# A two-layer encoder on one core: the residual kept in DRAM during the mixers, a step's values prepared after the step before it, and the mixer's modulation moved beside the inversions

## The chip, the cores and the metric

The kernel runs on one core of one Trainium2 chip. The metric is the device time of one execution in microseconds; the median of 3 runs is 1579.02 us (1576.25 to 1579.44). The names of the engines are those of the profile: PE (TensorE, matmuls), PEld (its weight loads), DVE (VectorE), ACT (ScalarE), POOL (GpSimd), SP (the queue that issues nearly all DMAs).

## The reference

Two layers, each of a half-step feed-forward, a gated mixer of three branches, and another half-step feed-forward; D = 1024, 256 tokens, hidden width 2816. All weights are float32.

```
def reference(x, c, ...):
    cs = silu(c)
    for l in range(2):
        mod = cs @ ada_w[l] + ada_b[l]                  # 9 vectors of 1024: shift, scale, gate of 3 sub-layers
        h = modulate(rmsnorm(x), sh1, sc1)
        x = x + 0.5 * gt1 * swiglu(h, ffn_wi[l, 0], ffn_wo[l, 0])
        h = modulate(rmsnorm(x), sh2, sc2)
        x = x + gt2 * hybrid_mixer(h, ...)
        h = modulate(rmsnorm(x), sh3, sc3)
        x = x + 0.5 * gt3 * swiglu(h, ffn_wi[l, 1], ffn_wo[l, 1])
    return rmsnorm(x, final_norm)

def hybrid_mixer(h, ...):
    proj = h @ w_in[l]
    o_a = dilated_attention(rotary(aq), rotary(ak), av)     # 8 heads x 64
    o_b = neighborhood_attention(nq, nk, nv, rpb[l])
    o_c = rwkv7_bidirectional(pr, pk, pv, ...)              # a scan over the tokens in each direction
    merged = sum of sigmoid(gate_b) * (o_b @ w_branch[b])   # over the three branches
    return merged @ w_out[l]

def _rwkv_step(state, inp):
    r, w, k, v, a_vec, b_vec = inp
    sa = state . a_vec
    state = state * w + sa (x) b_vec + v (x) k
    y = state . r
```

## The kernel before

The residual `xT` holds x transposed, 8 tiles of 128 x 256, in SBUF for the whole run. Every product is computed with float32 weights cut in two float32r parts: ACT casts a piece of 128 x 512 weights (`whi`, L360), DVE subtracts to get the rest (`wlo`, L369), and PE runs three matmuls for each 128 x 128 tile (L404 to L406, "dense matmuls" below). Weights come through SP in 512 KB loads (`wraw`).

The modulation is not done on PE. For each of the 72 blocks of 128 outputs of a layer SP loads 512 KB (`araw`) and DVE multiplies and sums them in one pass (L468). These loads are started by a pace: during a mixer 24 of them (vectors 5, 7 and 6 of the layer: the mixer's gate, the next scale, the next shift), from START = 110 after the mixer's start in the planner's clock, every PACE = 7.

The order of all instructions is fixed when the kernel is built. Each activity is a generator (a thread); `Order.run` gives every engine its next instruction by planned times, priorities and counted resources (`take`, `release`, `wait`). At run time every engine runs its list in order, and what arrives later than planned holds everything behind it on that engine. `s_big` counts the shared buffers of one pool (tag "b4", NBIG = 34), `s_z` smaller ones (NZ = 10). Thread `main` issues the dense matmuls; all else fits in between.

In the mixer the third branch (RWKV) is the long chain. Tokens are cut in four chunks of 64 in each direction (steps n = 0 to 3). For each step `invert` builds the chunk's matrices (`pG` on PE, `G` on DVE), inverts 8 x 8 blocks (`blocks8`: one matmul `p` at L1228, then 14 small DVE operations in a row) and doubles the block size three times (`pX`, `pT`, L1181 and L1193, with a copy, a predicated copy and a transposition between). `values` prepares what the scan needs of v and b (`pBT`, `pvt`, `pMV`; tiles `uv`, `bu`). `scan` then does the step itself (`pAS`, `pU`, `pS1`, `pY`), and `post` normalises the output (`pvar`, `pgi`) into `oC`. Only then can the third branch's product (`oC`), W_out (`m`) and the residual's update run. Two threads of `invert` run over steps 0, 2 and 1, 3; each takes five shared buffers for a step before it begins (G twice, `uv`, `bu`, `tw`), and `uv` and `bu` are held from there to the step's end:

```
for _ in range(5 - (n == 3) + (n == ns[0])):
    yield take(s_big)
...
G = [big("G", (128, 2, 4, 128)) for _ in range(2)]
uv = big("uv", (128, 2, 8, 64))
bu = big("bu", (128, 2, 8, 64)) if n < 3 else None
tw = big("tw", (128, 2, 2, 4, 64))
```

Beside the chain `main` runs the dense products of the projections, of the first two branches and of the gates (input `h` or `o`).

Of the kernel before, what the change touches and what calls it, by code (L numbers as in the profile page):

```python
# [8 lines left out]
F32 = mybir.dt.float32  # L9
# [12 lines left out]
BIG = 1e30  # L22
TWO_PI_PARTS = (6.28125, 0.0019350051879882812, 3.0199159819e-07)
ROUND = 12582912.0
NBIG, NZ, NZ2 = 34, 10, 2
NRAW, NSPL, NADA, NPM = 3, 4, 2, 3
ORDER = "cabAgB"
NCK, NLR = 2, 2
WARM = 0
NJ0 = 8  # L30
NXF, NXM = 4, 8
PACE, START = 7, 110
FPACE, FSTART = 5, 12
WPRIO = -1
LAT, MM = {"PE": 0.2, "ACT": 0.15, "DVE": 0.13, "SP": 0.0}, 0.329
VPRIO = 4
# [125 lines left out]
def wait(ev):  # L162
    return ("wait", ev, 0, 0)
# [6 lines left out]
def take(sem, n=1):  # L170
    return ("take", sem, n, 0)
# [20 lines left out]
def trunk(ctx, tc, A, out):  # L192
# [21 lines left out]
    def big(name, shape=(128, 4, S), dt=F32):  # L214
        return act.tile(list(shape), dt, name=name, tag="b4", bufs=NBIG)
# [7 lines left out]
    def free_big(n=1):  # L223
        od.release(s_big, n)
# [4 lines left out]
        eng.dma_start(t, A[key])  # L229
        return t  # L230

    xT = act.tile([128, KT, S], F32, name="xT")
    csb = const.tile([128, D], F32, name="csb")
    cT = cload("cT", [128, KT], eng=nc.sync)
    ident = cload("ident", [128, 128], eng=nc.sync)
# [271 lines left out]
    def mod(l, v):  # L507
        return modT[l][:, v * 8:v * 8 + 8]
# [344 lines left out]
    def mixer(l, st):  # L853
        yield take(s_big, 4)
        ha = Act("h", KT)
        od.spawn(modulated(l, 1, st, ha), 0)
        vec = tmp.tile([128, 14, 4], F32, name="vec", bufs=1)
        mul = tmp.tile([128, 2], F32, name="mul", bufs=1)
        for t, src in ((vec[:, 0:13], "vec"), (mul, "mul")):
# [262 lines left out]

        e_inv, e_val = ([Event() for _ in range(4)] for _ in range(2))
        CH = {}
        s_ck = Sem(NCK)
        n_inv, e_got = [0], [Event() for _ in range(5)]

        def toks(c):
            return slice(c * 64, c * 64 + 64)
# [1 line left out]
        def invert(ns):  # L1131
            for e in e_ab:
                yield wait(e)
            for n in ns:
                cs = (n, 3 - n)
                if n > 0:
                    yield wait(e_got[n - 1])
                yield take(s_ck)
                for _ in range(5 - (n == 3) + (n == ns[0])):
                    yield take(s_big)  # L1140
                od.set(e_got[n])
                if n == ns[0]:
                    tx = big("tx", (128, 2, 2, 4, 64))
                    T, X = tx[:, 0], tx[:, 1]
                G = [big("G", (128, 2, 4, 128)) for _ in range(2)]
                uv = big("uv", (128, 2, 8, 64))
                bu = big("bu", (128, 2, 8, 64)) if n < 3 else None
                tw = big("tw", (128, 2, 2, 4, 64))
                TT, W1 = tw[:, 0], tw[:, 1]
                for d in range(2):  # L1150
                    yield take(s_px, 2)
                    pp = [paux("pG", (128, 4, 128)) for _ in range(2)]
                    yield on("PE", 1.3)
                    for i in range(4):
                        for b in range(2):
                            hs = half(b)
                            P.matmul(pp[b][:, i], BK[d][i // 2][hs, i % 2, cs[d]].rearrange("p a b -> p (a b)"),
                                     ar_view(d, i // 2)[hs, :, i % 2, toks(cs[d])], start=True, stop=True)
                    for b in range(2):
                        yield on("DVE", 0.6)  # L1160
                        V.tensor_mul(G[b][:, d], pp[b], mg[:, d][:, None, :].to_broadcast([128, 4, 128]))
                        od.release(s_px)
                yield from blocks8(G, X, TT)
                yield on("DVE", 0.6)
                flip(T, TT)
                od.spawn(values(n, cs, G, bu, uv, W1), VPRIO)
                for lv in range(3):
                    w = 8 << lv

                    def part_(t, d, a):  # L1170
                        return t[:, d].rearrange("p h c -> p (h c)").rearrange("p (x a s) -> p x a s", a=2, s=w)[:, :, a]

                    def halves_(t, a):
                        return skew(part_(t, 0, a), part_(t, 1, 1 - a))

                    yield take(s_px)
                    px = paux("pX", (128, 2, 4, 64))
                    yield on("PE", 0.85)
# [12 lines left out]
                    for d in range(2):  # L1191
                        for h in range(8):
                            P.matmul(pt[half(h), d, h // 2], X[half(h), d, h // 2], TT[half(h), d, h // 2], start=True, stop=True)  # L1193
                    yield on("DVE", 0.335)
                    V.copy_predicated(halves_(TT, 1), lvl[:, lv].rearrange("p d (x s) -> p d x s", s=w), halves_(pt, 1))
                    od.release(s_px)
                    if lv < 2:
                        yield on("DVE", 0.6)
                        flip(T, TT)
                CH[n] = (G, bu, uv, TT, W1)  # L1200
                yield wait(e_val[n])
                od.set(e_inv[n])
            n_inv[0] += 1
            free_big(1 if n_inv[0] == 1 else 5)

        def blocks8(G, m, TT):

# [36 lines left out]

            V.transpose(t.rearrange("p d a b -> p (d a b)"), tt.rearrange("p d a b -> p (d a b)"))

        def values(n, cs, G, bu, uv, W1):
            for d in range(2):
                yield wait(e_rkv[d, 2])
            if n < 3:  # L1250
                yield take(s_px, 2)
                p = [paux("pBT", (128, 2, 4, 64)) for _ in range(2)]
# [26 lines left out]
            yield from copy_any(W1, p, 512)  # L1279
            od.release(s_px)  # L1280
            od.set(e_val[n])

        e_y = {(d, t): Event() for d in range(2) for t in range(2)}

        def scan():
# [2 lines left out]
            yield take(s_big)  # L1288
            for n in range(4):
                cs = (n, 3 - n)  # L1290
                yield wait(e_inv[n])
                G, bu, uv, TT, W1 = CH[n]
                ar = lambda d, h, z: ar_view(d, h // 4)[half(h), z, h // 2 % 2, toks(cs[d])]
# [52 lines left out]
                od.release(s_px)  # L1346
                free_big(5 - (n == 3))
                od.release(s_ck)
                ST = sn
            free_big(5)  # L1350

# [382 lines left out]
        ha.free()  # L1734
        yield take(s_big, 4)
        ma = Act("m", KT)
        yield wait(e_oC)
        yield from branch(2, oC[0], gts)
        free_big(4)
# [2 lines left out]
        yield wait(have[l, 5])  # L1742
        yield on("DVE", 0.07)
        V.tensor_scalar(g, mod(l, 5), 0.5, None, op0=OP.mult)
        p3 = []
        for m in range(NPM):
            yield take(s_pm)
# [23 lines left out]
    def main():  # L1771
# [14 lines left out]
        for k in range(KT):  # L1786
            yield on("DVE", 0.34)
            V.tensor_mul(xT[:, k], xT[:, k], st.r)
            if k % 2 == 0 or k == KT - 1:
                k0 = max(k - 1, 0) if k < KT - 1 else k  # L1790
                nc.sync.dma_start(out[:, k0:k + 1], xT[:, k0:k + 1])

    od.spawn(main(), 7, True)
# [124 lines left out]
```

## Time and profile before

| | |
|---|---|
| median of 3 runs | 1579.02 us |
| the profiled execution | 1579.55 us, its span 1577.7 us |
| busy in that span | PE 1509.2, PEld 1440.4, DVE 1288.8, ACT 856.1 us |
| mixer of layer 0, from its first normalisation (217.7 us) to the next (612.4 us) | 394.7 us |
| mixer of layer 1, 992.8 to 1384.3 us | 391.5 us |
| first chunk matrices (`pG`) in these | 391.6 us and 1155.5 us |

A window's row gives its length, then for each engine the busy time and the number of instructions that began in it; PEclk is the granted TensorE clock as a share of its full speed (1.00 is 2.4 GHz, 0.50 is 1.2 GHz), then the mean busy share of the DMA engines and GB/s. The two mixers are each cut at their first `pG` into a head (projections, attention) and a tail (inversions, scan, third branch, W_out).

### The profile page before, as it was taken

To read this page: it belongs to the slowest core of one execution; us is meant where nothing else is said; L and a number is where in the kernel's file an instruction comes from. 1 tells how busy PE (TensorE), PEld (TensorE's weight loads), DVE (VectorE), ACT (ScalarE), POOL (GpSimd) and SP (SyncE) were. 2 spreads that over 40 slices of the span, in tenths; PEclk is the share of its full clock that TensorE was granted. 3 is DMA by queue.
4 is the path that set the end of the run, shared out by engine and by line. 5 is a ranking of instruction groups with operands and counts; after the bars stand their busy time and mean duration, and the time that the engine had idled before them with its cause. 6 is when DMAs were issued, how large, how long until landed. Compare 5 with 4: busy or idle time off the path is not lost.

```text
span 1577.7 us, 36363 instructions
## 1 busy us (share of the span) xinstructions
PE 1509.2 (96%) x14470; PEld 1440.4 (91%) x14470; DVE 1288.8 (82%) x2732; ACT 856.1 (54%) x1730; POOL 2.3 (0%) x22
## 2 busy tenths in 40 slices
PE   6999999999899989999999999999999987999997
PEld 6998999979689879999999999998888977999997
DVE  8888789989768688988789877999897687998664
ACT  4556457566344347555565545676654433665554
POOL 0000000000000000000000000000000000000000
PEclk9999999999899969999999999999999988999999
DMA  9687864446223435887668885543652352457553
GB/s 345 215 301 269 277 224 162 163 147 234 100 95 133 135 139 196 274 289 262 221 208 278 276 273 195 189 159 129 219 165 100 122 190 106 146 202 267 188 187 121
DMA packets 96226, 311.58 MB, mean 197 GB/s; under 512 B 11444, under 2 KB 22964, under 8 KB 96056
## 3 DMA queue, kind: packets, MB, share of 16 engines
q1 hardware_dynamic: 95768, 309.15, 57.8%
q8 instruction: 113, 1.85, 0.5%
q14 instruction: 57, 0.47, 0.1%
q10 hardware_dynamic: 288, 0.10, 0.0%
HBM read 308.17 MB, written 1.05 MB: 196 GB/s over the span
## 4 chain that ended last, share of the span: by engine, by line
PE 88%; DVE 6%; DMA 3%; issue 1%; ACT 1%; SPq 1%; DVEq 0%; ACTq 0%
PE pmain L404 21%; PE pmain L405 20%; PE pmain L406 20%; DMA araw<-in_ada_w_dram 3%; PE pearly L404 2%; PE pearly L406 2%; PE pearly L405 2%; PE pX L1181 1%; DVE araw L468 1%; PE pT L1193 1%; PE pS L1499 1%; PE pfirst L405 1%; PE pfirst L406 1%; PE pfirst L404 1%; DVE wlo L369 1%
## 5 line engine op out<-in xcount | busy, mean ns | idle before, releaser
L360 ACT CAST whi<-wraw 128x512 fp32r<-128x512 f32 x828 | 508.5, 619 | 444.6 <-PE pmain L405 291.8
L369 DVE TENSOR_TENSOR wlo<-wraw,whi 128x512 fp32r<-128x512 f32 x828 | 566.6, 689 | 118.0 <-ACT whi L360 108.0
L404 PE MATMUL pmain<-h,whi 128*128 128x256 f32 x1840 | 528.1, 287 | 0.0
L405 PE MATMUL pmain<-h,whi 128*128 128x256 f32 x1840 | 517.4, 281 | 0.0
L406 PE MATMUL pmain<-h,wlo 128*128 128x256 f32 x1840 | 515.6, 280 | 0.0
L404 PEld LDWEIGHTS pmain<-h,whi 128*128 128x128 f32 x1840 | 346.1, 188 | 12.2 <-issue 8.2
L406 PEld LDWEIGHTS pmain<-h,wlo 128*128 128x128 f32 x1840 | 347.4, 189 | 0.3 <-DVE wlo L369 0.2
L405 PEld LDWEIGHTS pmain<-h,whi 128*128 128x128 f32 x1840 | 346.4, 188 | 1.1 <-issue 0.7
L468 DVE CUSTOM_DVE_ANT_0 araw<-araw,csb 128x1024 f32<-128x1024 f32 x144 | 174.7, 1218 | 47.1 <-DMA araw<-in_ada_w_dram 46.9
L406 PE MATMUL pmain<-z,wlo 128*128 128x256 f32 x704 | 198.5, 282 | 7.0 <-DVE wlo L369 7.0
L405 PE MATMUL pmain<-z,whi 128*128 128x256 f32 x704 | 198.4, 282 | 0.0
L404 PE MATMUL pmain<-z,whi 128*128 128x256 f32 x704 | 197.7, 281 | 0.0
L406 PEld LDWEIGHTS pmain<-z,wlo 128*128 128x128 f32 x704 | 132.8, 189 | 8.5 <-DVE wlo L369 8.4
L404 PEld LDWEIGHTS pmain<-z,whi 128*128 128x128 f32 x704 | 132.7, 189 | 0.0
L405 PEld LDWEIGHTS pmain<-z,whi 128*128 128x128 f32 x704 | 132.7, 188 | 0.0
L404 PE MATMUL pearly<-xh,whi 128*128 128x258 f32 x320 | 91.5, 286 | 0.0
L406 PE MATMUL pearly<-xh,wlo 128*128 128x258 f32 x320 | 90.4, 283 | 0.0
L405 PE MATMUL pearly<-xl,whi 128*128 128x258 f32 x320 | 90.1, 282 | 0.0
L405 PEld LDWEIGHTS pearly<-xl,whi 128*128 128x128 f32 x320 | 60.6, 189 | 0.0
L404 PEld LDWEIGHTS pearly<-xh,whi 128*128 128x128 f32 x320 | 60.6, 189 | 0.0
L406 PEld LDWEIGHTS pearly<-xh,wlo 128*128 128x128 f32 x320 | 60.4, 189 | 0.0
L427 ACT CAST z<-ffz 128x256 fp32r<-128x256 f32 x76 | 30.6, 405 | 35.2 <-DVE ffz L659 34.8
(301 smaller groups left out, 2369.8 us busy)
## 6 DMA issues: line engine op xcount, KB each, us to landing
wraw<-in_ffn_wi_dram SPq DMA_DIRECT2D x160, 512.0 KB, 4.6
araw<-in_ada_w_dram SPq DMA_DIRECT2D x144, 512.0 KB, 6.4
wraw<-in_ffn_wo_dram SPq DMA_DIRECT2D x88, 512.0 KB, 4.6
wraw<-in_w_in_dram SPq DMA_DIRECT2D x78, 512.0 KB, 4.0
wraw<-in_w_gb_dram SPq DMA_DIRECT2D x72, 512.0 KB, 3.8
w0raw<-in_ffn_wi_dram SPq DMA_DIRECT2D x16, 512.0 KB, 11.1
wraw<-in_w_out_dram SPq DMA_DIRECT2D x16, 512.0 KB, 3.7
bt<-in_bt_dram SPq DMA_DIRECT2D x16, 192.0 KB, 4.7
```

Of the source, the lines that this page charges most:

```text
L360: S_.copy(hi, part(q))
L369: V.tensor_tensor(lo, part(q), hi, op=OP.subtract)
L404: P.matmul(o, w[0], xh, start=first, stop=False)
L405: P.matmul(o, w[0], xl, start=False, stop=False)
L406: P.matmul(o, w[1], xh, start=False, stop=last)
L427: S_.copy(self.hi(k), src)
L468: V.tensor_tensor_reduce(out=raw, in0=raw, in1=csb, scale=0.5, scalar=0.0, op0=OP.mult, op1=OP.add, accum_out=modT[l][:, blk:blk + 1])
L1181: P.matmul(px[half(h), d, h // 2], G[h % 2][half(h), d, h // 2, 0:64], T[half(h), d, h // 2], start=True, stop=True)
L1193: P.matmul(pt[half(h), d, h // 2], X[half(h), d, h // 2], TT[half(h), d, h // 2], start=True, stop=True)
L1499: P.matmul(pS[e][:, t], qT[half(e), hp, t * 128:(t + 1) * 128], kT[half(e), hp], start=True, stop=True)
```

## The change

There are three parts. The residual: `xT` becomes two tiles of the shared pool (NBIG 36, NZ 8). When the mixer's normalisation has read it, SP stores the two halves to DRAM (`xs`) and the two buffers are free for the mixer; before W_out they are loaded again. The values: `uv` and `bu` are taken in `values`, one step at a time (NVL = 1), so that `invert` takes three buffers and no longer waits for the step's values; `scan` waits for both. The modulation: START 200 and PACE 5 in place of 110 and 7. The output is stored in five pieces as before, cut at other places.

```
-NBIG, NZ, NZ2 = 34, 10, 2
+NBIG, NZ, NZ2 = 36, 8, 2
-NCK, NLR = 2, 2
+NCK, NLR, NVL = 2, 2, 1
-PACE, START = 7, 110
+PACE, START = 5, 200
...
-    xT = act.tile([128, KT, S], F32, name="xT")
+    class Residual:
+        def __init__(self):
+            s_big.n -= 2
+            self.t = [big("xT") for _ in range(2)]
...
+    xs = [nc.dram_tensor(f"xs{l}", (128, KT, S), F32, kind="Internal").ap() for l in range(L)]
...
-        od.spawn(modulated(l, 1, st, ha), 0)
+        def norm():
+            yield from modulated(l, 1, st, ha)
+            for q in range(2):
+                yield on("SP", 1.45, 2.5)
+                nc.sync.dma_start(xs[l][:, 4 * q:4 * q + 4], xT.t[q])
+            xT.t = None
+            free_big(2)
+        def restore():
+            for _ in range(2):
+                yield take(s_big)
+            xT.t = [big("xT") for _ in range(2)]
+            for q in range(2):
+                yield on("SP", 1.45, 2.5)
+                nc.sync.dma_start(xT.t[q], xs[l][:, 4 * q:4 * q + 4])
+            od.set(e_x)
+        od.spawn(norm(), 0)
...
-                for _ in range(5 - (n == 3) + (n == ns[0])):
+                for _ in range(3 + (n == ns[0])):
...
-                CH[n] = (G, bu, uv, TT, W1)
-                yield wait(e_val[n])
                 od.set(e_inv[n])
...
+            if n > 0:
+                yield wait(e_vgot[n - 1])
+            yield take(s_vl)
+            for _ in range(1 + (n < 3)):
+                yield take(s_big)
+            od.set(e_vgot[n])
+            uv = big("uv", (128, 2, 8, 64))
+            bu = big("bu", (128, 2, 8, 64)) if n < 3 else None
+            CH[n] = (G, bu, uv, TT, W1)
...
+                yield wait(e_val[n])
                 yield wait(e_inv[n])
...
+                od.release(s_vl)
...
         ma = Act("m", KT)
+        od.spawn(restore(), 0)
...
+        yield wait(e_x)
```

PE's list at the end of the scan in layer 1, before: from the last step's `pAS` (the state's share) to the first product with `oC`.

```order
L1302 MATMUL pAS<-st,ar 64x64 x16
L1310 MATMUL pU<-tw 64x64 x16
L1337 MATMUL pY<-G,uv 64x64 x16
L1341 MATMUL pY<-ar,st 64x64 x16
L1402 MATMUL pvar<-c_sel,gsq 128x2 x8
L1420 MATMUL pgi<-c_ident,gsq 128x128 x8
L404 MATMUL pmain<-oC,whi 128x256
L405 MATMUL pmain<-oC,whi 128x256
L406 MATMUL pmain<-oC,wlo 128x256
```

PE's list after, from the last step's `pY` on (`pmain<-h` is a gate's dense product).

```order
L1379 MATMUL pY<-G,uv 64x64 x16
L1383 MATMUL pY<-ar,st 64x64 x16
L418 MATMUL pmain<-h,whi 128x256
L419 MATMUL pmain<-h,whi 128x256
L420 MATMUL pmain<-h,wlo 128x256
```

Before, 433 matmul rows of layer 1 stand without one dense matmul among them, from the last `p` (L1228) to `oC`; after, 300 dense matmuls stand between these two points, 66 of them behind the last `pY`. In layer 0 the same stretch has 120 dense matmuls before and 234 after, behind the last `pY` 0 and 60. The longest run without a dense matmul in a tail is 125 rows in layer 0 and 433 in layer 1 before, 48 and 52 after. The first `pG` stands behind 1080 and 1014 dense matmuls of its mixer before, behind 1005 and 909 after.

DVE's list in layer 1 before, from the state's update of step 2 to step 3's copy of `pU` (`araw` is a sum of the modulation, the row behind it reads the sum out; two more sums stand right ahead of this piece).

```order
L1329 TENSOR_TENSOR st_15849<-pS1_17586,st_15849 128x512
L1330 TENSOR_TENSOR st_15849<-st_15849,PC_13679 128x512
L468 ISA araw_17591,modT1_123<-araw_17591,csb_73 128x1024
L468 ISA modT1_123 128x1
L1195 COPY_PREDICATED tw_16940<-lvl_110,pT_17611 128x2x4x32
L486 TENSOR_TENSOR modT1_123<-modT1_123,c_ada_b_82 128x8
L1304 TENSOR_TENSOR tw_16940<-tw_16940,pAS_17685 128x512
L1312 COPY uv_16939<-pU_17703 64x8x64
```

DVE's list after, in layer 1 around the matrices of step 2.

```order
L1193 TENSOR_TENSOR G_16194<-pG_16197,c_mg_119 128x512
L482 ISA araw_16215,modT1_124<-araw_16215,csb_74 128x1024
L482 ISA modT1_124 128x1
L1193 TENSOR_TENSOR G_16193<-pG_16250,c_mg_119 128x512
L1421 SCALAR_TENSOR_TENSOR bon_15246<-bon_15246,vec_13211,pg_16246 128x256
L383 TENSOR_TENSOR wlo_16271<-wraw_15902,whi_16270 128x512
```

The sums moved from a close row in the scan's last two steps to places one by one between the step matrices and the weights' second parts. Of a mixer's 24 sums 17 and 20 stand behind the first `pG` before (layers 0 and 1), all 24 after, and 5 of these stand behind the last subtraction into `oC`, where none stood before.

SP's list around W_out's weights in layer 1, before.

```order
L345 DMA wraw<-in_w_gb_dram 128x1024 x5
L495 DMA araw<-in_ada_w_dram 128x1024
L345 DMA wraw<-in_w_out_dram 128x1024
L495 DMA araw<-in_ada_w_dram 128x1024 x12
L345 DMA wraw<-in_w_out_dram 128x1024 x7
L345 DMA wraw<-in_ffn_wi_dram 128x1024 x10
```

The same place after (with buffer numbers), with the residual's two loads.

```order
L887 DMA xT_17771<-xs1 128x1024
L359 DMA wraw_17779<-in_w_out_dram 128x1024
L509 DMA araw_17766<-in_ada_w_dram 128x1024
L887 DMA xT_17772<-xs1 128x1024
L509 DMA araw_17797<-in_ada_w_dram 128x1024
L509 DMA araw_17824<-in_ada_w_dram 128x1024
L359 DMA wraw_17857<-in_w_out_dram 128x1024
```

Twelve loads in a row are gone; two of the residual stand before and behind the first of W_out's weights.

## Rows read from the trace of the kernel before

**Rows 1.** The page: span, and busy time of each engine.

```profile
span 1577.7 us, 36363 instructions
PE 1509.2 (96%) x14470; PEld 1440.4 (91%) x14470; DVE 1288.8 (82%) x2732; ACT 856.1 (54%) x1730; POOL 2.3 (0%) x22
```

**Rows 2.** Windows: head and tail of the mixer, layer 0, then layer 1.

```profile
core 0: us, PE busy (x) PEld busy (x) DVE busy (x) ACT busy (x) POOL busy (x), PEclk, DMA share, GB/s
217.70:391.60 173.90, 173.90 (x1318) 157.07 (x1316) 158.79 (x349) 115.37 (x259) 0.00 (x0) 1.00 0.54 181
391.60:612.40 220.80, 200.81 (x2731) 184.39 (x2730) 169.03 (x383) 95.72 (x195) 0.00 (x0) 0.92 0.38 128
992.80:1155.50 162.70, 162.70 (x1220) 146.76 (x1218) 150.01 (x329) 105.61 (x235) 0.00 (x0) 1.00 0.52 174
1155.50:1384.30 228.80, 208.33 (x2829) 192.11 (x2829) 180.09 (x405) 103.44 (x219) 0.00 (x0) 0.95 0.40 136
```

**Rows 3.** Windows: the five stretches of the tails at half clock.

```profile
405.80:416.00 10.20, 8.95 (x32) 5.86 (x34) 8.73 (x32) 1.68 (x3) 0.00 (x0) 0.50 0.53 198
552.60:576.50 23.90, 16.58 (x114) 14.85 (x115) 18.13 (x41) 7.12 (x15) 0.00 (x0) 0.50 0.32 130
1293.30:1303.50 10.20, 7.10 (x96) 5.32 (x98) 9.53 (x29) 1.66 (x3) 0.00 (x0) 0.50 1.01 382
1330.80:1334.20 3.40, 3.20 (x54) 3.08 (x56) 0.00 (x0) 0.15 (x1) 0.00 (x0) 0.50 0.00 0
1337.60:1347.90 10.30, 7.93 (x33) 6.70 (x33) 7.35 (x20) 3.25 (x9) 0.00 (x0) 0.50 0.01 2
```

**Rows 4.** The chain that ended last, 540 to 570 us.

```profile
546.63 5.70 DMA araw<-in_ada_w_dram
552.35 1.22 DVE araw L468
...
560.66 1.13 DVE araw L468
...
565.59 1.14 DVE araw L468
...
567.40 1.13 DVE araw L468
```

**Rows 5.** DVE by line, 1300 to 1325 us: the costliest group.

```profile
L468 DVE CUSTOM_DVE_ANT_0 araw<-araw,csb 128x1024 f32<-128x1024 f32 x13 | 15.6, 1209 | 0.0
```

**Rows 6.** Timeline, end of layer 1's scan: the last `p`, the last `pY`, `oC`.

```profile
1293.92 2.07 PE L1228 MATMUL p<-tx,c_b 128*128 128x512 f32 x2 [2.89 <-DVE tx L1222]
...
1332.90 1.73 PE L1341 MATMUL pY<-ar,st 64*64 64x64 f32 x32
...
1342.15 0.58 PE L404 MATMUL pmain<-oC,whi 128*128 128x256 f32 x1 [1.41 <-ACT oC L1447]
```

**Rows 7.** Windows: inside layer 0's tail, and dense matmuls alone.

```profile
440.00:540.00 100.00, 98.14 (x1553) 91.45 (x1551) 72.74 (x162) 44.38 (x84) 0.00 (x0) 1.00 0.35 118
450.00:540.00 90.00, 89.64 (x1477) 83.88 (x1477) 64.37 (x141) 39.95 (x75) 0.00 (x0) 1.00 0.35 115
580.00:590.00 10.00, 10.00 (x87) 10.00 (x86) 9.82 (x28) 6.13 (x13) 0.00 (x0) 1.00 0.53 184
```

**Rows 8.** Windows: both tails' ends (third branch, W_out).

```profile
576.50:612.40 35.90, 35.90 (x305) 35.90 (x304) 32.74 (x75) 24.20 (x50) 0.00 (x0) 1.00 0.54 176
1347.90:1384.30 36.40, 36.40 (x310) 36.40 (x310) 32.94 (x76) 24.39 (x50) 0.00 (x0) 1.00 0.53 174
```

**Rows 9.** Tile araw in layer 0's tail: the sums, DVE's waits for loads, landing.

```profile
L468 DVE CUSTOM_DVE_ANT_0 araw<-araw,csb x17: 1173/1215/1226, 405.2 to 567.3; 128x1024 f32<-128x1024 f32 x17
...
  DMA araw<-in_ada_w_dram: 3.0, 2
...
DMA to landing us min/median/max: 5.6/6.5/8.1
```

**Rows 10.** DMA issues: a load and a store of the residual.

```profile
xT<-in_xT_dram SPq DMA_DIRECT2D x2, 512.0 KB, 4.4
...
out_dram<-xT SPq DMA_DIRECT2D x3, 256.0 KB, 2.4
```

More of the change, by code (lines that the diff above doesn't have):

```diff
@@ L230, in cload, with __getitem__ @@
         return t
-    xT = act.tile([128, KT, S], F32, name="xT")
+    class Residual:
+        def __init__(self):
+            s_big.n -= 2
+            self.t = [big("xT") for _ in range(2)]
+        def __getitem__(self, key):
+            k = key[1]
+            if isinstance(k, slice):
+                return self.t[k.start // 4][:, k.start % 4:(k.stop - 1) % 4 + 1]
+            return self.t[k // 4][:, k % 4]
+    xT = Residual()
+    xs = [nc.dram_tensor(f"xs{l}", (128, KT, S), F32, kind="Internal").ap() for l in range(L)]
     csb = const.tile([128, D], F32, name="csb")
@@ L855, in mixer @@
         ha = Act("h", KT)
-        od.spawn(modulated(l, 1, st, ha), 0)
+        e_x = Event()
+        def norm():
[14 more added lines that the diff above has]
+        od.spawn(norm(), 0)
         vec = tmp.tile([128, 14, 4], F32, name="vec", bufs=1)
@@ L1124, in mixer @@
         CH = {}
-        s_ck = Sem(NCK)
-        n_inv, e_got = [0], [Event() for _ in range(5)]
+        s_ck, s_vl = Sem(NCK), Sem(NVL)
+        n_inv, n_val, e_got, e_vgot = [0], [0], *([Event() for _ in range(5)] for _ in range(2))
         def toks(c):
@@ L1145, in invert @@
                 G = [big("G", (128, 2, 4, 128)) for _ in range(2)]
-                uv = big("uv", (128, 2, 8, 64))
-                bu = big("bu", (128, 2, 8, 64)) if n < 3 else None
                 tw = big("tw", (128, 2, 2, 4, 64))
@@ L1165, in invert @@
                 flip(T, TT)
-                od.spawn(values(n, cs, G, bu, uv, W1), VPRIO)
+                od.spawn(values(n, cs, G, TT, W1), VPRIO)
                 for lv in range(3):
@@ L1199, in invert @@
                         flip(T, TT)
-                CH[n] = (G, bu, uv, TT, W1)
-                yield wait(e_val[n])
                 od.set(e_inv[n])
-            n_inv[0] += 1
-            free_big(1 if n_inv[0] == 1 else 5)
+            free_big()
         def blocks8(G, m, TT):
@@ L1245, in flip, with values @@
             V.transpose(t.rearrange("p d a b -> p (d a b)"), tt.rearrange("p d a b -> p (d a b)"))
-        def values(n, cs, G, bu, uv, W1):
+        def values(n, cs, G, TT, W1):
             for d in range(2):
                 yield wait(e_rkv[d, 2])
+            if n > 0:
[7 more added lines that the diff above has]
+            CH[n] = (G, bu, uv, TT, W1)
             if n < 3:
@@ L1281, in values @@
             od.set(e_val[n])
+            n_val[0] += 1
+            if n_val[0] == 4:
+                free_big(4)
         e_y = {(d, t): Event() for d in range(2) for t in range(2)}
@@ L1788, in main @@
             V.tensor_mul(xT[:, k], xT[:, k], st.r)
-            if k % 2 == 0 or k == KT - 1:
-                k0 = max(k - 1, 0) if k < KT - 1 else k
+            if k % 2 == 1 or k > 5:
+                k0 = k - 1 if k < 6 else k
                 nc.sync.dma_start(out[:, k0:k + 1], xT[:, k0:k + 1])
```

## The prediction

> **What bounds the kernel now.** I read the page first: PE is busy 1509.2 of 1577.7 us, DVE 1288.8, ACT 856.1 [rows 1]. PE sets the time, so the question is where it is not at work at full clock. The page's 40 slices point to the two mixers; the windows by head and tail give the sizes. In both heads PE is busy for the whole stretch at clock 1.00, though DVE is 91 and 92% busy there (158.79 of 173.90, 150.01 of 162.70). In the tails PE is idle for 220.80 - 200.81 = 20.0 us and 228.80 - 208.33 = 20.5 us, and the mean clock is 0.92 and 0.95 [rows 2]. Five stretches of the tails ran at half clock (1.2 GHz). PE was busy 8.95 + 16.58 = 25.5 us in those of layer 0 and 7.10 + 3.20 + 7.93 = 18.2 us in those of layer 1 [rows 3]; at full clock that work takes half, so the clock cost at most 12.8 and 9.1 us. PE's work of a mixer at full clock is then 173.9 + 200.8 - 12.8 = 361.9 us, and 162.7 + 208.3 - 9.1 = 361.9 us: two counts that agree. The mixers take 394.7 and 391.5 us; 32.8 + 29.6 = 62.4 us is the most that a better order of them can return.
>
> What holds PE there is seen in the chain of waits: in layer 0 DVE stood 5.70 us before a modulation sum whose load was late, and three more sums lie on the chain up to 567 us [rows 4]. In layer 1 DVE did 13 such sums, 15.6 us, in 25 us of the scan's last steps [rows 5], and from the last `p` at 1293.9 us to `oC` at 1342.1 us PE had no dense matmul left in its list [rows 6]. The lists show the same without times: 433 rows in a row without a dense matmul.
>
> **The modulation and the buffers, taken together** because they have one answer: the new order of the tail. No arithmetic is removed. After it, 234 and 300 dense matmuls stand between the last `p` and `oC`, in place of 120 and 0; at 10 us for 87 of them [rows 7] the 300 are 34 us of PE, to which the small matmuls of that stretch come. The chain there took 48.2 us with 13 sums among it, and most of these are ahead of it now. So the waits of this stretch lose their cause, and with them most of the half clock. Of the 62.4 us I take all as returned and then charge what the new order costs:
>
> (a) Waits in a covered tail. Where dense matmuls stood among the small ones PE lost 0.36 us in 90, or 1.86 in 100 with the step's start included, at clock 1.00 [rows 7]. The tail up to the last `pY` is about 160 to 175 us of PE (361.9 less the head, less the end), so 0.6 to 3.3 us a mixer; I take the middle, 1.9, and 3.8 for both.
>
> (b) DVE in the end stretch. Third branch and W_out took 35.9 us with DVE at 32.74 [rows 8]. Five sums of 1.215 us [rows 9] now fall into it: 32.74 + 6.1 = 38.8 us, 2.9 above PE's time if DVE never waits, 6.7 above at the 91% at which it worked there (38.8 / 0.912 = 42.6). Middle 4.8, both mixers 9.6. Here nothing hides it: behind each sum the weights' second parts and the residual's updates are queued on DVE, and PE waits for these.
>
> (c) The hand-over to `oC`. From the last `pY`'s end at 1334.6 us to the first `oC` product PE waited 7.5 us through the normalisation (partly at half clock) [rows 6]. Now 60 and 66 dense matmuls lie there, 6.9 and 7.6 us. But DVE also has weights' second parts and gate products in this stretch. 0 to 5 us each; I take 2.5, both 5.
>
> (d) The clock. One stretch at half clock costs 3.6 to 4.5 us (half of the 7.10 and 8.95 us of work in the stretches of 10.2 us) [rows 3]. I charge one for both mixers, 4 us; bounds 0 and 8.
>
> (e) The residual's journey. Per mixer two stores and two loads of 512 KB. A load of the same tile landed in 4.4 us, a store of 256 KB in 2.4 us [rows 10], and the DMA engines are 38 to 54% busy there [rows 2]. The stores are read by nobody for over 200 us. The loads' cover is the third branch's products and the first half of W_out on three accumulators. If SP stands before a load until its buffer is free, the weights of W_out and `araw` loads queue behind it; three `wraw` buffers are the reserve. I take 0; without cover the first updates of the residual would come one load later, 4.4 us a mixer, 8.8 in all; below 0 it cannot be, since it only adds. The wait of a step's values for the step before, the fewer small buffers and the recut output change no row that a term rests on; they go into (a).
>
> The loads of `araw` landed after a median of 6.5 us, yet DVE waited only 3.0 us in 17 sums of the tail [rows 9]; I charge no more than (a).
>
> Sum: 3.8 + 9.6 + 5 + 4 = 22.4 us given back, 62.4 - 22.4 = 40.0 us gained. The profiled execution took 1579.55 us, so 1539.5; the median of the runs is 0.5 lower, so 1539. All terms at their good ends (1.2 + 5.8) give 1524, all at their bad ends (6.6 + 13.4 + 10 + 8 + 8.8 = 46.8) 1563.
>
> Against this speaks that PE's dense work is now cut into pieces of 3 to 24 matmuls between small ones of 64 x 64. The rows say that this mixture holds the clock: 100 us of it at 1.00 [rows 7]. The Trainium skill, Perfetto Trace Analysis, section Matmul Optimizations, says that the matmul engine scales its power with its use, so that matmuls should run back to back in batches; by that rule the spread order could keep the clock low, which is the first rival below. The trace agrees for the bare chain only, where the clock did fall.
>
> **The rivals.**
>
> The clock stays low in the tails although the waits go. For it: it fell in both tails, and no small matmul goes. Against: rows 7. Then the 21.9 us of the clock do not come back, and (d) is in it: 1539 + 21.9 - 4 = 1557.
>
> DVE's pace is the bound (the slower side). In the tails DVE was busy only 169.03 of 220.80, 76.6%, and 180.09 of 228.80, 78.7% [rows 2]. If that is not idleness for want of work but the pace that its chain of short dependent operations allows, the new order, which puts more on DVE behind the first `pG`, is slower. The first `pG` comes 75 and 105 dense matmuls earlier, 9 and 12 us, so the heads take 165 and 151 us and DVE does 151 and 139 us in them at the heads' pace. Of 327.8 and 330.1 us in all there remain 177 and 191 for the tails, which at 76.6 and 78.7% take 231 and 243 us: mixers of 396.3 and 393.6, together 3.7 us more than before, 1583. It decides from a tail pace below 77% in layer 0 and 79% in layer 1. Against it: with PE never waiting DVE ran at 91 and 92% in the heads, and in the bare chain DVE waits for PE and ACT.
>
> PE's busy time hides more waiting than its idle time shows. Weight loads are busy only 184.39 of 220.80 and 192.11 of 228.80 us in the tails; their gaps are 36.4 and 36.7 us, 32.6 us more than the idle time of the matmul row [rows 2]. If that were all waiting, 1539 - 32.6 = 1506. Against it: in layer 0's head the same gap is 16.8 us, where no wait is seen and the clock is full. The Trainium skill, Perfetto Trace Analysis, section Identifying the Most-Contended Engine, says just this, that matmul busy time is no measure of the distance to the best and the weight loads' share is the better one; by it the sum would end nearer 1506. The heads bear it out only as far as small matmuls load fewer weights.
>
> That the change doesn't do what it says can be left out: the lists show the dense matmuls and the sums moved.
>
> **How the numbers follow.** Forecast 0.79; clock stays low 0.08; DVE's pace 0.09; hidden waiting 0.04. About 0.2% (3 us) is what a measurement can tell from no change. Faster takes the forecast, the clock's case and the hidden waiting (0.91). DVE's pace at 1583 lies just beyond the bound on the slower side; I give it 0.06 slower and 0.03 within. The range is the forecast's own, 1524 to 1563, a little wider below for part of the hidden waiting and above for a late residual: 1520 to 1564. What is left out above is mainly DVE's pace.
>
> **What would show it.** The windows of both tails should have PE idle under 10 us, and the clock at 0.97 or more; the long row of `araw` sums at the scan's end should be gone, and dense matmuls stand beside `pAS` to `pgi`. (b) is right if PE waits for the weights' second part or the residual between `oC` and the next normalisation, with DVE near 100%. (e) is wrong if the residual's update waits for a load of `xT`. The prediction is wrong as a whole if DVE in the tails is still under 80% and PE idle by 20 us each, or if the half-clock stretches still add up to over 40 us.

## The result and the profile after

The changed kernel took a median of 1556.91 us (four runs, 1551.61 to 1559.27), the kernel before 1578.42 beside it: a ratio of 0.9861, 95% interval 0.9831 to 0.9891, so 21.5 us less. The forecast was 1539, and the time lies inside the range of 1520 to 1564: the sign is right, the gain about half of the 40 us. The profiled execution of the changed kernel is the fastest of its four, 1551.61 us; against 1579.55 of the one before that is 27.9 us. The sums below are made with these two executions; the 5.3 us between the profiled run and the median have no trace. The mean granted clock of the profiled execution was 0.992, that of the other three 0.983 to 0.990, so part of the 5.3 us may be clock; that is not shown.

The page of the changed kernel, span and busy time, as in [rows 1]:

```profile
span 1549.8 us, 36388 instructions
PE 1506.1 (97%) x14470; PEld 1436.0 (93%) x14470; DVE 1285.0 (83%) x2736; ACT 858.5 (55%) x1732; POOL 2.3 (0%) x22
```

The instructions are the same in number on PE. The windows of the mixers, cut at the same places as in [rows 2]: head and tail of layer 0, then of layer 1.

```profile
core 0: us, PE busy (x) PEld busy (x) DVE busy (x) ACT busy (x) POOL busy (x), PEclk, DMA share, GB/s
216.10:376.50 160.40, 160.40 (x1201) 145.21 (x1199) 144.56 (x321) 104.74 (x235) 0.00 (x0) 1.00 0.51 164
376.50:594.60 218.10, 208.93 (x2843) 190.63 (x2843) 181.13 (x411) 106.35 (x221) 0.00 (x0) 0.98 0.48 162
976.30:1124.50 148.20, 148.20 (x1091) 133.48 (x1089) 134.06 (x290) 95.74 (x211) 0.00 (x0) 1.00 0.50 162
1124.50:1356.00 231.50, 223.25 (x2958) 204.43 (x2958) 193.60 (x445) 115.97 (x243) 0.00 (x0) 0.98 0.48 162
```

The mixers take 378.5 and 379.7 us, 16.2 and 11.8 less than before; this is all of the 27.9. The heads are 13.5 and 14.5 us shorter. The tails hold 112 and 129 more PE instructions than before, in 2.7 us less and 2.7 us more. PE's idle time there fell from 20.0 and 20.5 us to 218.10 - 208.93 = 9.2 and 231.50 - 223.25 = 8.3. Of the five stretches at half clock in [rows 3] two are left, one in each mixer:

```profile
544.70:554.90 10.20, 6.90 (x27) 6.14 (x28) 6.71 (x16) 2.44 (x6) 0.00 (x0) 0.50 0.67 239
1305.90:1316.10 10.20, 6.88 (x26) 5.74 (x27) 7.43 (x18) 2.16 (x5) 0.00 (x0) 0.50 0.71 261
```

Both lie where the scan hands over to `oC`. The tails cut once more, at the first `oC` product and after `oC` has come through:

```profile
376.50:546.20 169.70, 165.52 (x2517) 148.77 (x2516) 138.82 (x313) 80.55 (x168) 0.00 (x0) 1.00 0.45 150
...
1124.50:1308.70 184.20, 179.77 (x2629) 162.73 (x2628) 150.78 (x346) 90.90 (x192) 0.00 (x0) 0.99 0.45 150
...
557.00:594.60 37.60, 34.46 (x284) 33.67 (x284) 35.03 (x83) 23.14 (x48) 0.00 (x0) 1.00 0.62 210
1318.00:1356.00 38.00, 35.87 (x294) 34.84 (x294) 35.67 (x84) 23.18 (x48) 0.00 (x0) 1.00 0.61 208
```

In the last two rows, the stretches of [rows 8], PE now stands for 3.1 and 2.1 us where it never stood before, and DVE is busy 93 and 94% of the time in place of 91 and 90%. The chain that ended last shows DVE there, and at the hand-over:

```profile
540.76 6.38 DMA araw<-in_ada_w_dram
...
547.16 1.23 DVE araw L482
...
567.87 1.13 DVE araw L482
569.01 1.14 DVE araw L482
...
572.78 1.22 DVE araw L482
```

A piece of a chain is not a wait of its own length. DVE's timeline shows what the 6.38 us were (last column: the idle time ahead, and what ended it):

```profile
541.83 1.22 DVE L482 CUSTOM_DVE_ANT_0 araw<-araw,csb 128x1024 f32<-128x1024 f32 x1
...
544.91 0.42 DVE L1492 TENSOR_TENSOR oC<-rkv,oC 128x256 fp32r<-128x256 f32 x1
...
546.37 0.42 DVE L1492 TENSOR_TENSOR oC<-rkv,oC 128x256 fp32r<-128x256 f32 x1
547.16 1.23 DVE L482 CUSTOM_DVE_ANT_0 araw<-araw,csb 128x1024 f32<-128x1024 f32 x1 [0.38 <-DMA araw<-in_ada_w_dram]
...
548.32 0.42 DVE L1492 TENSOR_TENSOR oC<-rkv,oC 128x256 fp32r<-128x256 f32 x1
...
550.00 0.42 DVE L1492 TENSOR_TENSOR oC<-rkv,oC 128x256 fp32r<-128x256 f32 x1 [0.47 <-ACT oC L1490]
```

DVE stood 0.38 us for the load; before that it had worked. My reading is that the sums cost by their own 1.2 us each: they stand in DVE's order among the operations that make `oC`, and behind `oC` (567.87 us and on) among the weights' second parts. The experiments test the second of these; the first stays open (see (c) below). In layer 1 DVE stood 1.01 us for a load ahead of its last operation on `oC` and 1.04 us for one behind it.

What the tails gained is seen in the timeline of the inversions. The row is the start, the duration, and the first product of a step, `pG`; before, layer 0's first and second step:

```profile
391.58 1.16 PE L1157 MATMUL pG<-ar,bk 64*128 64x128 f32 x16
...
432.73 1.16 PE L1157 MATMUL pG<-ar,bk 64*128 64x128 f32 x16
```

After the change:

```profile
376.50 2.06 PE L1189 MATMUL pG<-ar,bk 64*128 64x128 f32 x32
382.04 1.16 PE L1189 MATMUL pG<-ar,bk 64*128 64x128 f32 x16
```

The second step began 41.1 us after the first; now it begins 5.5 us after it, and in layer 1 7.3 us in place of 59.5. Two inversions run side by side, and one has work for PE where the other waits.

### The profile page after: what moved, and what is told of

Same layout as the page of the kernel before. It is cut to its first block, busy times and chain, and to the rows that moved or that the text cites. A ratio compares the mean times of both kernels' runs of the same rounds, so it can differ in the third digit from the quotient of the medians.

```text
span 1549.8 us, 36388 instructions
## 1 busy us (share of the span) xinstructions
PE 1506.1 (97%) x14470; PEld 1436.0 (93%) x14470; DVE 1285.0 (83%) x2736; ACT 858.5 (55%) x1732; POOL 2.3 (0%) x22
## 3 DMA queue, kind: packets, MB, share of 16 engines
q8 instruction: 113, 1.85, 0.5%
## 4 chain that ended last, share of the span: by engine, by line
PE 91%; DMA 3%; DVE 3%; issue 1%; ACT 1%; SPq 0%; DVEq 0%; ACTq 0%
PE pmain L418 22%; PE pmain L419 21%; PE pmain L420 21%; DMA araw<-in_ada_w_dram 3%; PE pearly L418 2%; PE pearly L419 2%; PE pearly L420 2%; PE pX L1213 2%; PE pT L1225 2%; PE pG L1189 1%; PE pS L1542 1%; PE po L1582 1%; PE pfirst L419 1%; PE pmain L1698 1%; PE pfirst L420 1%
## 6 DMA issues: line engine op xcount, KB each, us to landing
w0raw<-in_ffn_wi_dram SPq DMA_DIRECT2D x16, 512.0 KB, 10.9
```

## The experiments

**Which part makes the gain?** The change has three: the values' part of a step, the residual in DRAM with its two buffers, and the modulation's place. My theory was that they have one answer, the new order of the tail, with the modulation's dense matmuls as the cover; the rival, that one part alone does it. First the modulation's numbers alone (150, since the kernel before has no order for 200 with its buffers), and the change without them.

```
 e1_modulation_alone, against the kernel before
-PACE, START = 7, 110
+PACE, START = 5, 150
 e2_modulation_undone, against the changed kernel
-PACE, START = 5, 200
+PACE, START = 7, 110
```

> The kernel before with PACE, START = 5, 150 in place of 7, 110, nothing else (at START 200 its planner finds no buffers and stops). Theory (the gain is dense matmuls put among the scan's last steps; where the sums stand decides only if the chain is bare): its list has 0 dense matmuls from the last p to oC in layer 0 (433 bare rows) and 216 in layer 1, so layer 0's tail should lose about 30 us as layer 1's did before, layer 1's some 15 to 20: 1565 to 1575 in all. Rival (the sums' places are the gain, the buffers matter little): 1550 to 1560, as the changed kernel.

> The changed kernel with PACE, START = 7, 110 again: residual and values stay. 276 and 306 dense matmuls from the last p to oC, no sum behind oC, 4 to 7 sums in the heads. Theory: the cover alone makes the gain, and without sums in the end stretch it is a little larger than the change's: 1545 to 1557. Rival (the modulation's move is the gain): 1570 or more.

The residual back in a tile of its own, and the values' code as before (also at 150):

```
 e3_residual_undone, against the changed kernel
-    xT = Residual()
+    xT = act.tile([128, KT, S], F32, name="xT")
-NBIG, NZ, NZ2 = 36, 8, 2
+NBIG, NZ, NZ2 = 34, 10, 2
 e4_values_undone, against the changed kernel
-                for _ in range(3 + (n == ns[0])):
+                for _ in range(5 - (n == 3) + (n == ns[0])):
...
+                yield wait(e_val[n])
                 od.set(e_inv[n])
-PACE, START = 5, 200
+PACE, START = 5, 150
```

> The changed kernel with xT in its own SBUF tile again (34 shared and 10 small buffers, no store or reload); values and modulation stay. 258 and 261 dense matmuls from the last p to oC, 1 and 0 sums behind oC, but 244 and 149 bare rows at one place. Theory: 1550 to 1562, since the cover is there but a bare piece of 244 rows costs what the reload costs. Rival 1 (the reload on SP makes the loads behind it late and is what is left of the loss): 1540 to 1548. Rival 2 (without the two buffers the order falls back): 1568 or more.

> The changed kernel with values' buffers taken by the inversion again, five for a step, and START 150 (at 200 its planner stops for want of buffers); residual stays in DRAM. 387 and 399 dense matmuls from the last p to oC, all sums before the last copy of pU, bare pieces of 164 and 85 rows. Theory: with the cover and no sum in the end stretch 1540 to 1555, so the values' part is not needed. Rival (values' part is what lets steps overlap): 1565 or more.

Then the values' part and the residual each by itself, at the old 7, 110: `f1_values_alone` is e3's edit and `f2_residual_alone` e4's, both with

```
-PACE, START = 5, 200
+PACE, START = 7, 110
```

> The kernel before with the values' part alone changed: the residual stays in its own tile, the modulation keeps its old pace, the buffers are 34 and 10 as before. Theory A, the parts add up (values undone 1592, residual undone 1565, modulation undone 1556 against 1557 for the change): the values' part alone gives about 13 us, so 1563 to 1570. Theory B, the values' part needs the two freed buffers to start its step early: without them it waits for buffers as before and the time stays within 5 us of 1579, with 18 us or more of idle TensorE left in the stretch from the first pG to oC of the second mixer.

> The kernel before with the residual in DRAM during the mixers alone (36 big buffers, 8 others): the step still takes five buffers at once and the values' part follows its own step, and the modulation keeps its old pace. Theory A, two more buffers alone buy nothing, because the second step's inversions stand behind the first one's values: 1575 to 1585. Theory B, the buffers are what the first steps lacked: under 1570. A part of the 1592 of the run with the values undone was its early and dense modulation then, which this run takes away.

The lag is from the first step's first `pG` to the second step's, PE's idle time is from the first `pG` to the first `oC` product, each for layers 0 and 1, from the profiled execution. A ratio is to the kernel before, run beside each group of kernels: its median was 1578.4 us beside the change, 1579.5 beside e1 to e4, 1581.9 beside f1 to f3 and e5, 1580.5 beside the runs h1 to h4. So kernels of different groups are compared by their ratios.

| kernel | values | residual | modulation | median us | ratio to before (95%) | lag us | idle us |
|---|---|---|---|---|---|---|---|
| before | - | - | 7, 110 | 1578.4 | 1 | 41.1, 59.5 | 19.9, 20.3 |
| e1 | - | - | 5, 150 | 1582.7 | 1.0019 (1.0004 to 1.0035) | 58.8, 56.2 | 19.1, 18.2 |
| f2 | - | yes | 7, 110 | 1575.8 | 0.9961 (0.9944 to 0.9978) | 30.3, 51.2 | 19.6, 19.6 |
| e4 | - | yes | 5, 150 | 1592.2 | 1.0068 (1.0044 to 1.0093) | 43.5, 54.6 | 24.3, 23.8 |
| f1 | yes | - | 7, 110 | 1556.9 | 0.9833 (0.9808 to 0.9858) | 9.5, 16.3 | 9.8, 8.7 |
| e3 | yes | - | 5, 200 | 1564.6 | 0.9893 (0.9866 to 0.9919) | 4.8, 45.8 | 10.9, 15.9 |
| e2 | yes | yes | 7, 110 | 1555.9 | 0.9840 (0.9819 to 0.9861) | 3.0, 3.5 | 7.9, 4.0 |
| after | yes | yes | 5, 200 | 1556.9 | 0.9861 (0.9831 to 0.9891) | 5.5, 7.3 | 4.2, 4.4 |

The values' part alone gives the whole of the gain (f1), and no kernel of the table without it gains more than 0.4%. Theory B of f1 falls: the values' part does not need the freed buffers at the old pace. Theory A was too small: it adds up the parts to 1563 to 1570, and f1 took 1556.9. f2 came out as its theory A had it. The modulation's move alone gives nothing (e1, expected 1565 to 1575: a miss; the heads got 13.6 and 14.7 us shorter and the tails 14.1 and 18.7 longer), and on top of the rest nothing either (e2). e4 was expected at 1540 to 1555 and is slower than before: the theory that the dense matmuls are the cover falls with it. The lags and the idle time go with the time: where the second step starts 30 us or more late, PE is idle for 15 to 24 us in that layer, where it starts early for 4 to 11. Without the residual in DRAM (e3) the ratio is 0.3% higher than the change's and the time is above the 1550 to 1562 expected, but the two intervals overlap, so a loss is not shown by the time; the lag of 45.8 us is one sign of it, in layer 1.

**Which piece of the values' part?** It does two things: it takes two of a step's buffers later, and an inversion no longer waits for its own step's values.

```
 h1_take_early, against e2_modulation_undone
-                for _ in range(3 + (n == ns[0])):
+                for _ in range(5 - (n == 3) + (n == ns[0])):
...
-            for _ in range(1 + (n < 3)):
-                yield take(s_big)
             od.set(e_vgot[n])
```

> The changed kernel with the modulation at its old pace (7, 110), where it ran at 1556, and with one piece of the values' part undone: a step takes its five buffers at the start of its inversions again, not three there and two at its values. The waits stay as changed. Theory A, the later taking is what the values' part gains by (two steps' inversions hold 8 buffers together instead of 12): the time goes back to that of the residual alone, 1570 to 1580. Theory B, the gain comes from the wait that an inversion no longer makes for its own step's values: the time stays at 1553 to 1560.

1571.03 us, ratio 0.9942 (0.9928 to 0.9955), against 0.9840 of e2, as theory A had it: some 16 us of e2's gain go with this one piece. The lag is back, in layer 0 and in layer 1 (51.2 us):

```profile
393.40 1.16 PE L1189 MATMUL pG<-ar,bk 64*128 64x128 f32 x16
...
425.49 1.16 PE L1189 MATMUL pG<-ar,bk 64*128 64x128 f32 x16
```

Taking 3 buffers at the start (and one more for a worker's first step) lets two steps in with 8; with 5 they need 12. That is the mechanism, shown for the later taking. What dropping the wait does is small or nothing: h1, in which the wait is dropped, is at 0.9942, and f2, which has neither piece, at 0.9961 (0.9944 to 0.9978); the intervals overlap. Whether the later taking would do as much with the old wait in place, no run shows.

**What do the sums behind `oC` cost?** In the program's order five of the modulation's sums stand behind the last `oC` in each mixer.

```
 f3_start180, against the changed kernel
-PACE, START = 5, 200
+PACE, START = 5, 180
```

> The changed kernel with the modulation's start at 180 in place of 200: in the program's order 0 and 2 of the modulation's sums stand behind the last oC of the two mixers, where 5 and 5 stood. If those sums are what lengthens the end stretch (48.4 and 47.3 us from oC to the end, against 42.7 and 42.1 before), it shrinks by 4 to 5 us in the first mixer and 2 to 3 in the second, and the time falls to 1545 to 1552. Rival: the VectorE has the same work in either place and the sums come late in the stretch ahead of oC instead: the end shrinks, the stretch ahead of it grows by as much, and the time stays at 1554 to 1560.

1544.30 us, ratio 0.9761 (0.9739 to 0.9784): the theory, and a little more. The end stretch from `oC` went from 48.4 and 47.3 to 43.3 and 42.0 us, the stretch from the first `pG` to `oC` hardly changed (171.3 and 184.1, against 169.7 and 184.2), so the sums were paid for ahead of `oC` with 1.6 us in layer 0 at most. The windows that answer to those of the changed kernel from 557 and 1318 us:

```profile
564.00:597.00 33.00, 33.00 (x280) 33.00 (x279) 29.95 (x69) 22.39 (x47) 0.00 (x0) 1.00 0.60 188
1316.00:1348.50 32.50, 32.15 (x273) 31.94 (x272) 30.43 (x73) 22.44 (x47) 0.00 (x0) 1.00 0.61 191
```

PE is idle 0.0 and 0.35 us there. This kernel beats the one before and the changed one.

**Does the residual's reload hold SP's queue up?** In the changed kernel the reload is issued just ahead of the load at 540.76 us that the chain names, by SP's timeline. (I had read the chain's 6.38 and 5.96 us as waits when I wrote what this run should show.)

```profile
540.33 0.38 SPq L887 DMA_DIRECT2D xT<-xs  x1
540.76 0.42 SPq L509 DMA_DIRECT2D araw<-in_ada_w_dram  x1
...
544.06 0.42 SPq L887 DMA_DIRECT2D xT<-xs  x1
544.54 0.91 SPq L509 DMA_DIRECT2D araw<-in_ada_w_dram  x2
```

```
 e5_restore_pool, against the changed kernel; h2_pool180 the same with START 180
-                nc.sync.dma_start(xT.t[q], xs[l][:, 4 * q:4 * q + 4])
+                nc.gpsimd.dma_start(xT.t[q], xs[l][:, 4 * q:4 * q + 4])
```

> The changed kernel with the reload of the residual issued from GpSimd's queue in place of SyncE's. If the reload holds up the loads that stand behind it on SyncE (the modulation's weights whose sums VectorE waits for ahead of oC, 6.38 and 5.96 us of the chain), these loads are issued and land earlier: the half-clock window at oC (10.2 us in each mixer) shrinks or goes, and the time falls by 4 to 8 us, to 1548 to 1553. Rival: the loads are late by their own issue and the landing of 5 to 6 us, whatever queue the reload takes: the waits ahead of oC stay at 5 us or more and the time is within 2 us of 1557.

> The changed kernel with both: the modulation's start at 180, which gave 1544 alone, and the residual's reload from GpSimd's queue, which gave 1551 alone. Theory A, two separate waits, so the gains of 12 and 5 us add in part: 1537 to 1543. Rival: with the sums out of the end stretch, loads are no longer what VectorE waits for there, so the queue of the reload is worth nothing more: 1543 to 1547.

e5 took 1551.21 us, 0.9807 (0.9781 to 0.9833); its interval overlaps that of the changed kernel (0.9831 to 0.9891), so a gain of its own is not shown. DVE's waits for `araw` loads in the tails fell from 5.7 and 3.8 us to 2.0 and 2.3, so the loads behind the reload did come earlier; the half clock stayed in both mixers. But PE's wait for the first `oC` product in layer 0 is as long in e5 as in the changed kernel (3.82 us), so it was not these loads that PE waited for:

```profile
552.33 0.58 PE L418 MATMUL pmain<-oC,whi 128*128 128x256 f32 x1 [3.82 <-ACT oC L1490]
```

Of the waits that the reload could have lengthened, only 0.38 us in layer 0 and 1.01 in layer 1 stand ahead of DVE's last operation on `oC`; the longest, 2.57 us, stands behind it, for a load issued at 544.54, behind the reload's second half. With the start at 180 no gain is seen: h2 at 1547.05, 0.9784 (0.9771 to 0.9798), against 0.9761 of f3.

**Does the residual in DRAM pay at a better pace?**

```
 h3_residual_undone180 is e3_residual_undone with
-PACE, START = 5, 200
+PACE, START = 5, 180
```

> The changed kernel with the modulation's start at 180 and the residual back in its own tile (34 and 10 buffers). Theory A, the two extra buffers pay only where the modulation is dense beside the inversions: in the program's order 244 and 149 matmuls of the mixers' own work then run with nothing of the modulation between them, against 48 and 52, so half-clock windows and idle come back and the time is 1555 to 1565, against 1544. Rival, the residual in DRAM adds nothing at any pace (as at the old one, where both were at 1556): 1542 to 1548.

1560.58 us, 0.9873 (0.9859 to 0.9886), against 0.9761 with the residual in DRAM: about 17 us, as theory A had it. The loss is in layer 1, where the second step's `pG` comes late again; the first and the second step of h3:

```profile
1120.06 1.16 PE L1155 MATMUL pG<-ar,bk 64*128 64x128 f32 x16
...
1165.78 1.16 PE L1155 MATMUL pG<-ar,bk 64*128 64x128 f32 x16
```

In f3 the second step starts 7.3 us after the first:

```profile
1122.43 1.16 PE L1189 MATMUL pG<-ar,bk 64*128 64x128 f32 x16
...
1129.74 1.06 PE L1189 MATMUL pG<-ar,bk 64*128 64x128 f32 x16
```

The same 40 us of both, the row of h3 and then that of f3:

```profile
1160.00:1200.00 40.00, 29.45 (x426) 22.92 (x423) 27.53 (x75) 12.54 (x34) 0.00 (x0) 0.83 0.31 99
```

```profile
1160.00:1200.00 40.00, 39.93 (x719) 34.95 (x718) 30.02 (x65) 17.60 (x42) 0.00 (x0) 1.00 0.39 129
```

With the modulation late, the first `pG` comes earlier, and in layer 1 the two buffers decide whether the second step gets in beside it. At the old pace they add nothing (f1 against e2).

**The last sums ahead of `oC` too:**

```
 h4_pool175, against h2_pool180
-PACE, START = 5, 180
+PACE, START = 5, 175
```

> As the run with start 180 and the reload on GpSimd's queue, with the start at 175: none of the modulation's sums stands behind the last oC of either mixer (0 and 1 there). If each sum behind oC still costs about 1.2 us of VectorE in the end stretch, 1 to 2 us less than that run; the rival is that 5 and 5 more sums ahead of oC delay oC itself, and it is 2 to 5 us more.

1543.56 us, 0.9768 (0.9754 to 0.9781), against 0.9784 of h2: the intervals overlap, and it is level with f3. The rival (2 to 5 us more) is out; whether the one sum that is left costs its 1 to 2 us these runs cannot tell.

## Why the prediction came out as it did

**What bounds the kernel** was read rightly: PE, with its idle time and half clock in the tails. The terms against the trace of the changed kernel, both mixers together:

| term | charged us | measured us | from |
|---|---|---|---|
| (a) waits in the covered tail | 3.8 | 0.4 | idle of the tails, 17.4, less the next two rows |
| (b) DVE in the end stretch | 9.6 | 5.2 | idle from 557 and 1318 us on: 3.1 + 2.1 |
| (c) hand-over to `oC` | 5.0 | 11.8 | PE's waits for `oC`, and in layer 1 for the normalisation ahead of it: 3.82 and 2.8 + 1.6 ahead of the first product; idle 1.85 and 1.7 behind it |
| (d) half clock | 4.0 | 6.9 | half of 6.90 and 6.88 |
| (e) the residual's journey | 0 | 0 | no update waited for a load of `xT` |
| PE's own work longer | 0 | 10.1 | 369.3 - 3.45 and 371.45 - 3.44, less 361.9 each |
| sum | 22.4 | 34.4 | 62.4 - 34.4 = 28.0; the trace has 27.9 |

**The step that failed** is the one ahead of the terms: "PE's work of a mixer at full clock is then 361.9 us", taken as fixed for any order. The same instructions cover 365.9 and 368.0 us of busy time in the changed kernel. Worked out in the same way it was 361.6 and 363.0 with the steps apart in h1, and 365.8 and 365.7 with them together in f3; but f1 had 362.6 in layer 0 with the steps together, so it does not go with the lag alone. Most of it lies in the dense matmuls: the time that `pmain` covers in a mixer, its half-clock part taken at half, grew from 230.7 and 230.1 us to 234.4 and 236.6.

The trace shows where most of it can come from. A dense product that stands next to a small one takes longer until the next product starts: here 0.21 us behind the row at 529.83 and 0.22 behind that at 532.20, and 0.12 behind that at 532.42.

```profile
529.83 0.28 PE L420 MATMUL pmain<-h,wlo 128*128 128x256 f32 x1
530.04 1.15 PE L1379 MATMUL pY<-G,uv 128*64 128x64 f32 x32
...
532.20 0.39 PE L418 MATMUL pmain<-h,whi 128*128 128x256 f32 x1
532.42 0.28 PE L419 MATMUL pmain<-h,whi 128*128 128x256 f32 x1
532.54 0.28 PE L420 MATMUL pmain<-h,wlo 128*128 128x256 f32 x1
```

PE goes from dense to small products or back 137 and 123 times in the two mixers before, and 161 and 155 times after. Over the mixers of both traces, from start to start and with the half-clock part at half, a dense product takes 0.21 us at such a change and 0.12 to 0.13 elsewhere, a small one 0.12 and 0.05 (small ones of different shapes taken together). That is about 0.15 us a change, so 24 and 32 more of them make some 3.7 and 4.9 us, of the 4.0 and 6.1 by which the work grew. This is worked out and not shown by a run: none changed this number alone, and f1's first mixer, with 155 changes at 362.6 us, does not fit. The whole term is 10.1 of the 12.1 us by which the profiled execution misses the forecast.

**(a), (b), (c).** Their sum was right, 17.4 against 18.4 us; the parts were not, so that is luck. (c) is over its bound of 5 in both layers (5.7 and 6.1 us): the cover of 60 and 66 dense matmuls was there, but PE waited 3.82 us for the first `oC`, while DVE went through sums, second parts and gate products. The step named these last two as what is in the way and left out the sums, of which four in each mixer stand between the scan's last update and the last `oC` by the program's order. But the cover was too short even without them. Where no sum stands at this place, PE stood there 4.0 and 3.5 us behind 78 dense matmuls (f1's second mixer, e2's first), 2.3 us behind 114 (e2's second) and not at all behind 162 (f1's first). What the four sums add to this is left open, since no run takes them away and keeps the cover.

The prediction also read a piece of the chain as a wait. The 5.70 us of [rows 4] were 2.81 us of standing:

```profile
552.35 1.22 DVE L468 CUSTOM_DVE_ANT_0 araw<-araw,csb 128x1024 f32<-128x1024 f32 x1 [2.81 <-DMA araw<-in_ada_w_dram]
```

And of the 7.5 us that (c) took for PE's wait in layer 1 before, PE was busy with the normalisation's own products for 4.0. In the changed kernel the waits for the sums' loads grew, in layer 0's tail to 5.7 us in all from the 3.0 of [rows 9], for 24 sums in place of 17; the longest, 2.57 us, came behind `oC`:

```profile
L482 DVE CUSTOM_DVE_ANT_0 araw<-araw,csb x24: 1174/1218/1226, 438.5 to 572.8; 128x1024 f32<-128x1024 f32 x24
...
  DMA araw<-in_ada_w_dram: 5.7, 5
...
DMA to landing us min/median/max: 5.0/5.9/9.2
```

The mechanism of (b) is shown by f3, which takes all but two of the sums away and has PE idle there for 0.35 us in all. Its price is more than the idle time of 3.1 + 2.1 us: f3 is about 16 us faster by the ratios, 9.1 by the profiled mixers (376.2 and 372.9 us), and its end stretches alone are 5.1 + 5.3 us shorter.

**(d)** The clock fell once in each mixer, not once in both, at the same hand-over, so it came with (c). In f1's first mixer, where PE did not stand at this place, the clock did not fall there. Here PE stood just before and between these products:

```profile
546.15 0.58 PE L418 MATMUL pmain<-oC,whi 128*128 128x256 f32 x1 [3.82 <-ACT oC L1490]
```

**(e)** was right at 0, though the journey was longer than [rows 10] let expect: by the page the store of 512 KB landed after 8.6 us and the reload after 6.9. The cover held. What I missed is the other side of the residual: the two buffers are worth about 17 us at the start of 180 (h3), and nothing at the old pace.

**The modulation and the buffers as one.** Here the prediction had a time inside its range for a wrong reason. It took the dense matmuls behind the last `p` as what ends the waits. They bring nothing by themselves: e4 had 387 and 399 of them there by the program's order, its PE idle time was 24.3 and 23.8 us, and it was slower than the kernel before. What ends the waits ahead of the hand-over is that two steps' inversions run together, and what lets them is the later taking of two buffers, for which the prediction had only a clause ("go into (a)"). The modulation's place then decides where its sums fall.

**The rivals.** The clock did not stay low: 0.98 in both tails. That its 1557 is the measured time is chance. DVE's pace is no bound: 181.13 of 218.10 and 193.60 of 231.50 us are 83 and 84%, above the 77 and 79% below which the change would have lost by it, and f3 went to 84 and 86% (180.72 of 214.60 and 193.38 of 226.10 us). The weight loads' gaps fell from 36.4 and 36.7 us to 27.5 and 27.1, by 8.9 and 9.6, less than the idle time itself (10.8 and 12.2): no hidden waiting came back. The rule that the Trainium skill gives in Perfetto Trace Analysis, section Identifying the Most-Contended Engine, that matmul busy time is no measure of the distance to the best, is borne out in another way than the rival had it: the busy time of the same matmuls moved by 4 to 6 us a mixer.

## What to carry to other kernels

When a pipelined stage stands still, look first at what its second step holds and takes before it may begin: taking two of five buffers at the place where they are first written was worth some 16 of the 25 us that e2 gained, where dense filler beside a lone chain brought none. Filler then has to end before the hand-over: its last operations stand in an engine's order ahead of what the next stage waits for, and starting it at 180 in place of 200 gave some 16 us on top of the 21.5, by the ratios. Do not take an engine's busy time as its floor under another order, and do not take a piece of the chain as a wait before the engine's own timeline shows the idle time.

## What was not expected of the hardware

The busy time of the same PE instructions at full clock grew from 361.9 us to 365.9 and 368.0 when two chains of small matmuls and the dense ones were interleaved, and most of this growth can be put down to 24 and 32 more changes between small and dense products. The granted clock held 1.00 and 0.99 through 169.70 and 184.20 us of this mixture, and in this kernel's mixers fell to half only where PE had waited at `oC`.
